# Parts of a head's sums loaded ahead of its attention and summed between projections; eight modulation tiles moved into the first layer's heads

## The chip, the cores and the metric

One core of a Trainium2 chip runs the whole program once per execution. The metric is the time of an execution on the device in microseconds. TensorE (PE) multiplies, VectorE (DVE) and ScalarE (ACT) do the elementwise work, GpSimd (POOL) helps, and SyncE (SP) issues all the DMAs of this kernel from one queue, in order. Every engine takes its instructions in one fixed order, which is set when the kernel is built: a scheduler simulates the program in time and lists, for each engine, what became ready first, by the order in which the program was written.

## The reference

Two layers over 1024 prompt tokens and 8 x 8 sample tokens, width 1024, 8 heads of 128. Each layer is a modulated RMS norm, a mixer with a gate path, an output projection and a gated residual. The modulation (shift, scale and gate, 3 x 1024 columns) is one product of the conditioning vectors with `ada_w`. Layer 0's mixer is a gated delta rule, layer 1's is attention in three dilated groups whose outputs are combined with weights from their log-sum-exponents:

```python
mod = einsum('bd,de->be', silu(c), ada_w) + ada_b
shift, scale, gate = split(mod, 3)
h = rms_norm(x, norm_g) * (1 + scale) + shift
x = x + gate * mixer(h)            # gated_delta_rule in layer 0, dilated attention in layer 1
...
for gi, (window, dil) in enumerate(((128, 1), (512, 4), (2048, 16))):
    o, lse = dilated_attn(q[gi], k[gi], v[gi], window, dil)
wts = softmax(stack(lses))         # over the three groups
o = sum(wts * stack(outs))         # the "sum" of a head
y = (o * silu(z)) @ w_out
```

## The kernel before, in words

A projection (`project`) is one tile of 128 output columns over all 1088 tokens: three chunks of 384, 384 and 320 tokens, each 24 products (8 blocks of the depth, times three products of the split operands: high by high, high by low, low by high). The weights come in by `wraw` (512 KB, two buffers in turn), ACT rounds them to `whi` and DVE or POOL subtracts to get `wlo` (two buffers each). A chunk's result stands in one of two PSUM banks `pp` until it is copied out.

A modulation tile (`ada_tile`) is 128 columns of `ada_w`: eight products written as 16 PE instructions with the conditioning vectors (L153), a copy by ACT (L155), a folding product (L160) and a bias by DVE (L166 to L170). Its 512 KB of weights come through `wraw` too. 24 such tiles stand in a list, and each convolution projection of layer 0's heads (24 of them, `conv_tile`, all but one) calls `ada.pump(1)`, which runs one tile. The last eight tiles, the gates of layer 1, were loaded through a pool of their own, `ap` (L142), and run at the end of layer 0, one behind each of eight blocks of the last modulation (`modulate`, L1086).

In layer 0 the scheduler gives PSUM banks named `ps` (two) in the order of the program. The program's order at the start is: the key projection of head 0 with its system (`stage_k`), its query and value projections (`stage_qv`), the key projection of head 1, and then the scans.

Layer 1 runs four pairs of heads; in each pair the groups g = 2, 1, 0, and in each group the two heads (a = 0, 1): three projections (v, k, q), then `attention`, which yields block by block. PE fills the waits of one head's attention with the next head's projections. After each projection come `qk.pump`, `pv.pump` (the sample tokens' work) and `cmb.pump(2)`. The outputs of groups 2 and 1 go to DRAM (`gscr`). When a head's group 0 is done, `combine` is put into `cmb`: for each half of the tokens it loads the two parts into two buffers `stgc` (L1254), does the sum on DVE and ACT (L1257 to L1275), transposes it on PE (L1279), copies it back into a `stgc` buffer (L1281) and stores it to `oscr` (L1282). The transposes are ordered behind the newest product of a projection (`newest[0]`). The gate path (`z_head`) reads `oscr` at the end of the layer.

Of the kernel before, what the change touches and what calls it, by code (L numbers as in the profile page):

```python
# [8 lines left out]
F32 = mybir.dt.float32  # L9
# [5 lines left out]
P = 128  # L15
# [27 lines left out]
def kernel(ctx, tc, I, O):  # L43
# [58 lines left out]
    def wraw(src, n=P):  # L102
        t = wp.tile([P, KD, P], F32, name="wraw", bufs=2)
        SY.dma_start(out=t[:, :, :n], in_=src.rearrange("(k p) n -> p k n", p=P))
        return t
# [30 lines left out]
                        next(woven[0], None)  # L136
            cb(ci, acc)

    def ada_load(layer, ct, pool, ahead):
        src = I["ada_w"][layer, :, ct * P:(ct + 1) * P]  # L140
        t = pool.tile([P, KD, P], F32, name="aw", bufs=ahead)
        SY.dma_start(out=t, in_=src.rearrange("(k p) n -> p k n", p=P))  # L142
        return t

    def ada_tile(layer, ct, w):
        ada_fold(layer, ct, ada_rows(w))

# [92 lines left out]
            if not self.todo:  # L240
                self.credit = 0.0

    def ada_tiles(pool, todo):
        def load(i):
            layer, ct = todo[i]
            return ada_load(layer, ct, pool, 2) if pool else wraw(I["ada_w"][layer, :, ct * P:(ct + 1) * P])
        w = load(0) if pool else None
        for n, (layer, ct) in enumerate(todo):
            nxt = load(n + 1) if pool and n + 1 < len(todo) else None
            ada_tile(layer, ct, w if pool else load(n))  # L250
            w = nxt
            yield

    ada = Units()
    ada.todo.append(ada_tiles(None, [(0, c) for c in range(16, 24)] + [(1, i + o) for i in range(8) for o in (8, 0)]))


    W0 = I["a_w_in"][0]
# [290 lines left out]
    def conv_tile(t, dst):  # L549
        w = wsplit(wraw(W0[:, t * P:(t + 1) * P]), G if 8 <= t < 16 else V)  # L550
        prev = [None]

        def cb(ci, acc):
            cn = CHUNKS[ci][1]
            xin = sb.tile([P, 387], F32, name="xin", bufs=2)
            if ci == 0:
                G.memset(xin[:, 0:3], 0.0)
            else:
                G.tensor_copy(out=xin[:, 0:3], in_=prev[0][:, 384:387])
            prev[0] = xin  # L560
            if ci < 2:
                A.copy(out=xin[:, 3:3 + cn], in_=acc[:, :cn])
                W = cn
            else:
                A.copy(out=xin[:, 3:259], in_=acc[:, :256])
                xs = xin[:, 259:347].rearrange("p (b x) -> p b x", x=11)
                G.tensor_copy(out=xs[:, :, 0:3], in_=scT[:, t, :].rearrange("p (b i) -> p b i", i=3))
                A.copy(out=xs[:, :, 3:11], in_=sview(acc[:, 256:320]))
                W = 344
                cst = sb.tile([P, 27], F32, name="cst", bufs=2)  # L570
                G.tensor_copy(out=cst[:, 0:3], in_=xin[:, 256:259])
                G.tensor_copy(out=cst[:, 3:27].rearrange("p (b i) -> p b i", i=3), in_=xs[:, :, 8:11])
                ct = acc[:27, 320:320 + P]
                PE.transpose(ct, cst, ident)
                cso = sb.tile([27, P], F32, name="cso", bufs=2)
                V.tensor_copy(out=cso, in_=ct)
                SY.dma_start(out=conv_p[:, t * P:(t + 1) * P], in_=cso[0:3, :])
                SY.dma_start(out=conv_s[:, t * P:(t + 1) * P], in_=cso[3:27, :])
            ca = sb.tile([P, 387], F32, name="ca", bufs=2)
            A.activation(out=ca[:, :W], in_=xin[:, 0:W], func=AF.Copy, scale=cwT[:, 0, t:t + 1])  # L580
            for i in range(1, 4):
                stt(ca[:, :W], xin[:, i:i + W], cwT[:, i, t:t + 1], ca[:, :W], ALU.mult, ALU.add)
            th = xin
            A.activation(out=th[:, :W], in_=ca[:, :W], func=AF.Tanh)
            c0 = CHUNKS[ci][0]
            if ci < 2:
                stt(dst[:, c0:c0 + cn], th[:, :cn], 1.0, ca[:, :cn], ALU.add, ALU.mult)
            else:
                stt(dst[:, c0:NP], th[:, :256], 1.0, ca[:, :256], ALU.add, ALU.mult)
                v1 = th[:, 259:347].rearrange("p (b x) -> p b x", x=11)[:, :, 0:8]  # L590
                v2 = ca[:, 259:347].rearrange("p (b x) -> p b x", x=11)[:, :, 0:8]
                stt(sview(dst[:, NP:]), v1, 1.0, v2, ALU.add, ALU.mult)
        project(w, hh, hl, cb)
        if t != 8:
            ada.pump(1)

    def banks_natural(src):
        out = []
# [409 lines left out]
    first.close()  # L1008
    set_banks(ctx, ps=3, lv=2, sc=1)

    aps = ExitStack()
    ap = aps.enter_context(tc.tile_pool(name="ap", bufs=1, reuse_waits="tile"))
    zp = ExitStack()
    zpool = zp.enter_context(tc.tile_pool(name="zp", bufs=1, reuse_waits="tile"))
    oh[7], ol[7] = (zpool.tile([P, T], F32R, name=n) for n in ("oh7", "ol7"))
# [47 lines left out]
    x1scr = [dr.tile([P, T], F32, name=f"x1scr{j}") for j in range(KD)]  # L1063
    x1 = [Columns("hh", F32) for _ in range(KD)]
    hh, hl = new_h()
    ada.todo.append(ada_tiles(ap, [(1, c) for c in range(16, 24)]))
    with tc.tile_pool(name="mid", bufs=1, reuse_waits="tile") as mp:
        def norm(qs, b0, b1):
            rn = col_stats(qs, b0, b1)
            rB = mp.tile([P, WIDE], F32, name="rB")  # L1070
            row_bcast(rB, rn, b0, b1)
            return rB

        def post(j):
            SY.dma_start(out=x1scr[j][:, :WIDE], in_=x1[j][:, :WIDE])

        def post2(j):
            SY.dma_start(out=x1scr[j][:, WIDE:], in_=x1[j][:, WIDE:])
            modulate(1, j, x1[j], rB, mp, hh, hl, 0, WIDE, True)
        qs = out_project(mp, 0, I["a_w_out"][0], xscr, x1, oh, ol, post, PASSES[0])  # L1080
        rB = norm(qs, 0, WIDE // P)
        qs = out_project(mp, 0, I["a_w_out"][0], xscr, x1, oh, ol, post2, PASSES[1])
        rB = norm(qs, WIDE // P, NC + 1)
        for j in range(KD):
            modulate(1, j, x1[j], rB, mp, hh, hl, WIDE, T, j % 2 and j < KD - 1)
            ada.pump(1)  # L1086
    zp.close()
    aps.close()
    l0.close()


# [45 lines left out]
    Z = [sd.tile([P, ZW * n], F32, name=f"Z{g}").rearrange("p (b x) -> p b x", b=2 * NB)  # L1137
         for g, n in enumerate((1, 4, 8))]
    for t in Z:
        V.memset(t, 0.0)  # L1140
    odS = sd.tile([P, 512], F32, name="odS")
    G.memset(odS, 0.0)
    comb = sd.tile([P, 4, NL], F32, name="comb")
# [18 lines left out]
    def proj_tile(g, part, h, dst, dsts):  # L1162
        col = ((part * NG + g) * NH + h) * P
        w = wsplit(wraw(W1_[:, col:col + P]))

        def cb(ci, acc):
            c0, cn = CHUNKS[ci]
            n = cn if ci < 2 else cn - NS
            todo = [(perm(dst, g, c0, n), pin(acc, g, n))]
            if ci == 2:  # L1170
                todo.append((dsts[:, h % 2, :], acc[:, n:cn]))
            for o, i in todo:
                if part == 0:
                    A.activation(out=o, in_=i, func=AF.Copy, scale=-SCALE)
                elif part == 1:
                    A.copy(out=o, in_=i)
                else:
                    V.tensor_copy(out=o, in_=i)  # L1178
        project(w, hh, hl, cb)

    def to_natural(src, nat, blocks, eng):
# [59 lines left out]
                A.copy(out=stg[:, b - 3:b + 1, 0:P], in_=v3(ob))  # L1241
            yield

    def combine(h, X0):

        for half in range(2):
            yield from combine_half(h, X0, half * 4)

    def combine_half(h, X0, n0):

        X = [X0[:, n0:n0 + 4, :]]
        for g in (1, 2):
            t = sb.tile([P, 4, 130], F32, name="stgc", bufs=2)
            SY.dma_start(out=t, in_=gscr[g - 1][h].rearrange("(n p) e -> p n e", p=P)[:, n0:n0 + 4, :])  # L1254
            X.append(t)
        yield
        d = sb.tile([P, NG, 4], F32, name="cd", bufs=1)  # L1257
        mm = sb.tile([P, 4], F32, name="cm", bufs=1)
        t = sb.tile([P, NG, 4], F32, name="ct", bufs=1)
# [11 lines left out]
        for n in range(4):  # L1271
            o = X[0][:, n, 0:P]
            A.activation(out=o, in_=o, func=AF.Copy, scale=d[:, 0, n:n + 1])
            for g in (1, 2):
                stt(o, X[g][:, n, 0:P], d[:, g, n:n + 1], o, ALU.mult, ALU.add)  # L1275
        yield
        tb = bank()
        for n in range(4):
            t = PE.transpose(tb[:, n * P:(n + 1) * P], X[0][:, n, 0:P], ident)  # L1279
            order_after(t, newest[0], "the sum is ready behind the products before")  # L1280
        A.copy(out=X[1][:, :, 0:P], in_=v3(tb))  # L1281
        SY.dma_start(out=oscr[h][:, n0 * P:(n0 + 4) * P].rearrange("p (n q) -> p n q", q=P), in_=X[1][:, :, 0:P])  # L1282

    def wide(tag, bufs, name=None, dtype=F32):

# [204 lines left out]
    for hp in range(4):  # L1490
        smd, vnew = [None] * NG, [None] * NG
        nmd = sd.tile([P, 4], F32, name="nmd", bufs=2)
        for g in (2, 1, 0):
            qTs, kTs, vTs = (sb.tile([P, 2, NS], F32, name=n, bufs=3) for n in ("qTs", "kTs", "vTs"))
            for a in range(2):
                h = 2 * hp + a
                vT = wide("vT", 1)
                kT = wide("kT", 2)
                qT = wide("qT", 2)
# [20 lines left out]
                if g == 1:  # L1520
                    SY.dma_start(out=scr.rearrange("(j p r) e -> p r j e", j=2, p=P),
                                 in_=stg.rearrange("p (r j) e -> p r j e", j=2))
                elif g == 2:
                    dv = scr.rearrange("(m rp r2) e -> r2 m rp e", rp=8, r2=2)
                    for r2 in range(2):
                        SY.dma_start(out=dv[r2], in_=stg[64 * r2:64 * r2 + 64])
                else:
                    cmb.todo.append(combine(h, stg))
                    cmb.pump(1)
        if hp < 3:  # L1530
            qk.todo.append(after(hp, smd, nmd, vnew))
# [70 lines left out]
```

## Time and profile before

| what | us |
|---|---|
| three runs, median (lowest to highest) | 2420.28 (2412.72 to 2430.17) |
| the profiled execution | 2412.29 |
| its span | 2410.6 |
| PE busy | 2250.9 (93%) |
| weight loads into PE busy | 2116.5 (88%) |
| DVE, ACT, POOL busy | 1375.5, 937.6, 257.6 |
| mean granted clock of PE | 0.962 |

By the order of time: to about 60 us the norm and modulation of layer 0; to about 835 its heads and gates; to about 970 its output projection and the norm and modulation of layer 1; to about 2235 the heads of layer 1; then gates and output. A matmul's end in the profile is modelled and overlaps the next one's start, so a busy PE is not PE at its peak. "[idle before <-releaser]" is how long the engine stood still just before the instruction, and what it had waited for.

### The profile page before, as it was taken

To read this page: it belongs to the slowest core of one execution; us is meant where nothing else is said; L and a number is where in the kernel's file an instruction comes from. 1 tells how busy PE (TensorE), PEld (TensorE's weight loads), DVE (VectorE), ACT (ScalarE), POOL (GpSimd) and SP (SyncE) were. 2 spreads that over 40 slices of the span, in tenths; PEclk is the share of its full clock that TensorE was granted. 3 is DMA by queue.
4 is the path that set the end of the run, shared out by engine and by line. 5 is a ranking of instruction groups with operands and counts; after the bars stand their busy time and mean duration, and the time that the engine had idled before them with its cause. 6 is when DMAs were issued, how large, how long until landed. Compare 5 with 4: busy or idle time off the path is not lost.

```text
span 2410.6 us, 43253 instructions
## 1 busy us (share of the span) xinstructions
PE 2250.9 (93%) x16647; PEld 2116.5 (88%) x16647; DVE 1375.5 (57%) x3414; ACT 937.6 (39%) x2477; POOL 257.6 (11%) x418
## 2 busy tenths in 40 slices
PE   7899889999999998999998999899998999999998
PEld 5788778788888997999898999899998999989897
DVE  6678767867784437336733555434655336375334
ACT  5445445455443325233233332333323333234234
POOL 2213322333221103100000000000000000000000
PEclk9889989899999999999999999999999999999998
DMA  9223222223333445448822697535966349786634
GB/s 314 69 74 86 76 68 76 79 69 91 79 87 89 120 149 162 131 146 265 272 66 71 218 301 246 167 100 183 332 222 211 98 143 337 198 267 180 203 101 149
DMA packets 482255, 379.42 MB, mean 157 GB/s; under 512 B 46206, under 2 KB 457071, under 8 KB 482048
## 3 DMA queue, kind: packets, MB, share of 16 engines
q1 hardware_dynamic: 482048, 376.65, 51.6%
q8 instruction: 131, 2.15, 0.4%
q14 instruction: 76, 0.62, 0.1%
HBM read 322.31 MB, written 54.27 MB: 156 GB/s over the span
## 4 chain that ended last, share of the span: by engine, by line
PE 65%; DMA 11%; DVE 11%; issue 7%; ACT 3%; POOL 1%; SPq 1%; POOLq 0%; ACTq 0%; DVEq 0%
PE pp L129 47%; PE ps L1238 2%; PE ps L1220 2%; DMA DT<-gcscr 2%; PE sc L1438 2%; DMA wraw<-in_a_w_in_dram 2%; DVE vtmp L713 2%; DMA qb<-qscr 1%; PE ps L1184 1%; DVE pr L1389 1%; PE ps L1229 1%; DVE ca L72 1%; DMA oscr<-stgc 1%; PE ps L153 1%; DMA out_y_p_dram<-yn 1%
## 5 line engine op out<-in xcount | busy, mean ns | idle before, releaser
L129 PE MATMUL pp<-hh,whi 128*128 128x384 f32 (+1 forms) x2688 | 914.3, 341 | 14.5 <-DVE vT L1178 5.8
L129 PE MATMUL pp<-hl,whi 128*128 128x384 f32 (+1 forms) x2688 | 904.0, 336 | 1.3 <-POOL hl L214 1.3
L129 PE MATMUL pp<-hh,wlo 128*128 128x384 f32 (+1 forms) x2688 | 900.8, 335 | 2.0 <-DVE wlo L111 2.0
L129 PEld LDWEIGHTS pp<-hh,whi 128*128 128x128 f32 x2688 | 512.5, 191 | 29.8 <-DVE vT L1178 8.5
L129 PEld LDWEIGHTS pp<-hl,whi 128*128 128x128 f32 x2688 | 512.8, 191 | 6.6 <-issue 1.9
L129 PEld LDWEIGHTS pp<-hh,wlo 128*128 128x128 f32 x2688 | 511.3, 190 | 7.7 <-issue 2.9
L111 DVE TENSOR_TENSOR wlo<-wraw,whi 128x1024 fp32r<-128x1024 f32 x136 | 171.2, 1259 | 131.3 <-ACT whi L110 130.5
L110 ACT CAST whi<-wraw 128x1024 fp32r<-128x1024 f32 x144 | 150.7, 1046 | 230.0 <-PE pp L129 148.2
L1225 ACT ACTIVATE sm<-sm,stg 128x128 f32<-128x128 f32 (+1 forms) x192 | 86.6, 451 | 340.4 <-DVE stg L1223 299.8
L1389 DVE TENSOR_TENSOR pr<-kc,qb 128x1024 f32<-128x1024 f32 x128 | 154.9, 1218 | 85.2 <-DMA qb<-qscr 55.7
L1379 DVE TENSOR_REDUCE ST<-pr 128x8 f32<-128x1024 f32 x128 | 153.7, 1213 | 1.1
L438 POOL TENSOR_TENSOR ol<-zo,oh 128x384 fp32r<-128x384 f32 x9 | 9.1, 1013 | 1311.4 <-ACT oh L437 1291.2
L72 DVE SCALAR_TENSOR_TENSOR ca<-xin,cwT,ca 128x384 f32<-128x384 f32 (+1 forms) x216 | 129.0, 601 | 7.1 <-ACT ca L580 5.9
L1223 DVE CUSTOM_DVE_ANT_0 sm<-ps,mA 128x256 f32<-128x256 f32 (+1 forms) x128 | 48.3, 377 | 139.4 <-PE ps L1220 138.2
L1238 PE MATMUL ps<-vnat,pT 128*128 128x128 f32 x560 | 97.1, 281 | 8.1 <-DVE pT L1234 6.4
L713 DVE TENSOR_TENSOR vtmp<-Vi,Mi 128x2 f32<-128x2 f32 (+30 forms) x248 | 99.0, 399 | 4.2 <-POOL so L88 0.7
L1238 PEld LDWEIGHTS ps<-vnat,pT 128*128 128x128 f32 x560 | 86.1, 190 | 14.3 <-issue 4.8
L1220 PE MATMUL ps<-kT,qT 128*128 128x128 f32 (+1 forms) x384 | 93.5, 325 | 1.2 <-DVE stg L1223 1.2
L1232 ACT COPY pT<-ps 128x256 f32<-128x256 f32 (+1 forms) x96 | 32.4, 337 | 119.3 <-PE ps L1229 118.4
L72 DVE SCALAR_TENSOR_TENSOR hh<-pp,GT,xr 128x384 f32<-128x384 f32 (+1 forms) x48 | 27.4, 571 | 82.4 <-PE pp L129 78.7
L129 PE MATMUL pp<-oh,whi 128*128 128x384 f32 (+1 forms) x216 | 71.7, 333 | 2.7 <-DVE zt L72 2.7
L129 PE MATMUL pp<-oh,wlo 128*128 128x384 f32 (+1 forms) x216 | 71.9, 334 | 1.5 <-DVE wlo L111 1.5
(449 smaller groups left out, 3556.1 us busy)
## 6 DMA issues: line engine op xcount, KB each, us to landing
qb<-qscr SPq DMA_DIRECT2D x128, 512.0 KB
kc<-in_cache_kv_w_dram SPq DMA_DIRECT2D x104, 512.0 KB
vc<-in_cache_kv_w_dram SPq DMA_DIRECT2D x104, 512.0 KB
wraw<-in_b_w_in_dram SPq DMA_DIRECT2D x80, 512.0 KB
wraw<-in_a_w_in_dram SPq DMA_DIRECT2D x32, 512.0 KB
wraw<-in_ada_w_dram SPq DMA_DIRECT2D x24, 512.0 KB
stgc<-gscr SPq DMA_DIRECT2D x32, 260.0 KB
aw<-in_ada_w_dram SPq DMA_DIRECT2D x8, 1024.0 KB
```

The lines of the kernel that those rows point to most:

```text
L72: return (eng or V).scalar_tensor_tensor(out=out, in0=in0, scalar=scalar, in1=in1, op0=op0, op1=op1)
L110: A.copy(out=hi, in_=raw)
L111: (eng or V).tensor_tensor(out=lo, in0=raw, in1=hi.bitcast(F32), op=ALU.subtract)
L129: mm = PE.matmul(acc[:, :cn], lhsT=a[:, k, :], rhs=b[k][:, c0:c0 + cn], start=(n == 0), stop=(n == 3 * KD - 1))
L713: V.tensor_tensor(out=tv, in0=Vi[:, :na, :w], in1=Mi[:, :w, c].unsqueeze(1).broadcast_to([P, na, w]), op=ALU.mult)
L1220: PE.matmul(sv, lhsT=qT[:, b * P:(b + 1) * P], rhs=kT[:, k0:k0 + w], start=True, stop=True)
L1223: V.tensor_tensor_reduce(out=sm[:, :w], in0=sv, in1=mk, scale=1.0, scalar=3e38, op0=ALU.add, op1=ALU.min, accum_out=stg[:, b, 128:129])
L1225: A.activation(out=sm[:, :w], in_=sm[:, :w], func=AF.Exp, scale=-1.0, bias=stg[:, b, 128:129], accum_out=stg[:, b, 129:130])
L1238: PE.matmul(ob[:, (b % 4) * P:(b % 4 + 1) * P], lhsT=pT[:, i * P:(i + 1) * P], rhs=vnat[:, k0 // P + i, :], start=(i == 0), stop=(i == w / ...
L1379: V.tensor_reduce(out=sv[:, n:n + 4, :], in_=pr.rearrange("p (n a e) -> p n a e", a=2, e=P), op=ALU.add, axis=AX.X)
L1389: V.tensor_tensor(out=out, in0=k, in1=q, op=ALU.mult)
L1438: mm = PE.matmul(od[32 * j:32 * j + 8, f * P:(f + 1) * P], lhsT=Z[g][:, a * NB + 2 * j + c, 8 * k:8 * k + 8], rhs=vc[:, j, a * P:(a + 1) * P],
```

## The change

- `combine` is put into `cmb` before the head's group 0 is projected, with an empty box. Its first step (after the projections of the head, or after the first one) loads the parts of the first half; it then yields until the head's own output is in the box. The sum of the first half follows directly behind the attention in the program, its transposes behind the next projection; the loads of the second half follow these, two more yields stand between, so its sum comes behind the second projection and its transposes behind the third.
- The eight gate tiles of layer 1 join the list of the 24; the calls behind three projections at the start (t = 0 and 16, query and value of head 0, and t = 9, key of head 1) run three tiles instead of one, 29 calls in all, and the last three tiles run where all that is left is run (`ada.pump(100)`, where one was left before). The pool `ap` goes.
- The tiles `Z` are cleared by POOL instead of DVE, and the value copies of the first projected head of layer 1 (group 2, head 0) are done by ACT instead of DVE.

```diff
-    def ada_load(layer, ct, pool, ahead):
...
-    ada.todo.append(ada_tiles(None, [(0, c) for c in range(16, 24)] + [(1, i + o) for i in range(8) for o in (8, 0)]))
+    ada.todo.append(ada_tiles([(0, c) for c in range(16, 24)] + [(1, i + o) for i in range(8) for o in (8, 0)]
+                              + [(1, c) for c in range(16, 24)]))
...
         if t != 8:
-            ada.pump(1)
+            ada.pump(3 if t in (0, 16, 9) else 1)
...
-    ada.todo.append(ada_tiles(ap, [(1, c) for c in range(16, 24)]))
...
             modulate(1, j, x1[j], rB, mp, hh, hl, WIDE, T, j % 2 and j < KD - 1)
-            ada.pump(1)
...
     for t in Z:
-        V.memset(t, 0.0)
+        G.memset(t, 0.0)
...
-                    V.tensor_copy(out=o, in_=i)
+                    (A.copy if (g, h) == (2, 0) else V.tensor_copy)(out=o, in_=i)
...
-    def combine(h, X0):
-        for half in range(2):
-            yield from combine_half(h, X0, half * 4)
...
+    def combine(h, box):
+        def load(n0):
+            parts = []
+            for g in (1, 2):
+                t = sb.tile([P, 4, 130], F32, name="stgc", bufs=2)
+                SY.dma_start(out=t, in_=gscr[g - 1][h].rearrange("(n p) e -> p n e", p=P)[:, n0:n0 + 4, :])
+                parts.append(t)
+            return parts
+        parts = load(0)
         yield
+        while not box:
+            yield
+        for n0 in (0, 4):
+            X = [box[0][:, n0:n0 + 4, :]] + parts
+            add_up(X)
+            yield
+            tb = bank()
+            for n in range(4):
+                t = PE.transpose(tb[:, n * P:(n + 1) * P], X[0][:, n, 0:P], ident)
+                order_after(t, newest[0], "the sum is ready behind the products before")
+            A.copy(out=X[1][:, :, 0:P], in_=v3(tb))
+            SY.dma_start(out=oscr[h][:, n0 * P:(n0 + 4) * P].rearrange("p (n q) -> p n q", q=P), in_=X[1][:, :, 0:P])
+            if n0 == 0:
+                parts = load(4)
+                yield
+                yield
+            yield
...
                 h = 2 * hp + a
+                if g == 0:
+                    box = []
+                    cmb.todo.append(combine(h, box))
...
                 else:
-                    cmb.todo.append(combine(h, stg))
+                    box.append(stg)
                     cmb.pump(1)
```

`add_up` is the body of the sum as it was (L1257 to L1275).

## Rows read from the trace of the kernel before

**Rows 1.** Page, part 1: busy us, share of span, instructions.
```profile
PE 2250.9 (93%) x16647; PEld 2116.5 (88%) x16647; DVE 1375.5 (57%) x3414; ACT 937.6 (39%) x2477; POOL 257.6 (11%) x418
```
**Rows 2.** PE's waits, 985 to 2235: us in total, times, longest.
```profile
PE ps L1279 <- DVE stg L72: 31.8, 5, 8.5
...
PE ps L1279 <- ACT knew L1326: 2.4, 1, 2.4
```
**Rows 3.** Order of time, PE: start us, us, instruction.
```profile
1291.43 0.45 PE L1279 MATMUL ps<-ident,stg 128*128 128x128 f32 x1 [6.04 <-DVE stg L72]
...
1544.71 0.44 PE L1279 MATMUL ps<-ident,stg 128*128 128x128 f32 x1 [8.33 <-DVE stg L72]
1544.95 1.91 PE L1184 MATMUL ps<-ident,vT 128*128 128x128 f32 x8
...
1908.56 0.45 PE L1279 MATMUL ps<-ident,stg 128*128 128x128 f32 x1 [4.62 <-DVE stg L72]
```
**Rows 4.** Order of time, SP, ACT and DVE beside these stalls.
```profile
1535.86 0.37 SPq L1282 DMA_DIRECT2D oscr<-stgc  x1
1538.38 0.36 SPq L1254 DMA_DIRECT2D stgc<-gscr  x1
...
1536.42 0.59 ACT L1241 COPY stg<-ps 128x512 f32<-128x512 f32 x1
1543.23 1.28 ACT L1273 ACTIVATE stg<-stg,cd 128x128 f32<-128x128 f32 x4 [1.18 <-DVE cd L1270]
...
1541.29 0.17 DVE L1261 TENSOR_TENSOR cm<-cm,stgc 128x4 f32<-128x4 f32 x1 [5.10 <-DMA stgc<-gscr]
...
1899.50 0.59 ACT L1241 COPY stg<-ps 128x512 f32<-128x512 f32 x1 [2.89 <-PE ps L1238]
```
**Rows 5.** Stage table, all work: window, us, busy by engine, granted clock, DMA.
```profile
1544.00:1546.00 2.00, 1.29 (x6) 1.32 (x7) 1.88 (x8) 0.50 (x2) 0.00 (x0) 0.50 0.00 0
...
1548.00:1550.00 2.00, 2.00 (x14) 2.00 (x15) 0.79 (x4) 0.57 (x3) 0.00 (x0) 0.94 0.61 182
```
**Rows 6.** Stage table of the seam: PE, PEld, DVE, ACT, POOL; then L129 alone.
```profile
951.90:971.60 19.70, 11.50 (x140) 8.17 (x129) 13.70 (x51) 7.67 (x25) 4.73 (x12) 0.65 0.72 212
...
951.90:971.60 19.70, 0.95 (x4) 0.69 (x5) 0.65 0.72 212
```
**Rows 7.** Order of time in the seam, PE, DVE and SP.
```profile
956.26 0.64 PE L153 MATMUL ps<-aw,cT 128*32 128x128 f32 x16 [2.51 <-DMA aw<-in_ada_w_dram]
...
951.97 0.49 DVE L72 SCALAR_TENSOR_TENSOR tmp<-hh,SC,rB 128x256 f32<-128x256 f32 x1 [0.28 <-ACT rB L226]
...
969.41 1.48 DVE L1178 COPY vT<-pp 128x384 f32<-128x384 f32 x2
...
952.11 13.93 SPq L142 DMA_DIRECT2D aw<-in_ada_w_dram  x6
```
**Rows 8.** Stage table, projections (L129) alone: window, us, PE, PEld, clock, DMA.
```profile
89.00:101.70 12.70, 11.41 (x65) 10.24 (x63) 1.00 0.32 61
...
101.70:123.00 21.30, 0.00 (x0) 0.00 (x0) 0.56 0.41 97
244.00:265.00 21.00, 0.00 (x0) 0.04 (x1) 0.83 0.23 64
```
**Rows 9.** Order of time in the seam, POOL clearing and DVE beside it.
```profile
966.21 0.32 POOL L1103 MEMSET mA<- 128x256 f32 x1
...
966.62 0.47 DVE L72 SCALAR_TENSOR_TENSOR tmp<-hh,SC,rB 128x256 f32<-128x256 f32 x1
```
**Rows 10.** Chain that ended last, 116 to 124: start us, us, what.
```profile
117.02 1.01 PE ps L153 x16
...
118.09 4.05 DMA wraw<-in_a_w_in_dram
...
122.16 1.04 ACT whi L110
```
**Rows 11.** Order of time, SP's queue at the start.
```profile
32.60 2.87 SPq L104 DMA_DIRECT2D wraw<-in_a_w_in_dram  x1
```

More of the change, by code (lines that the diff above doesn't have):

```diff
@@ L137, in project @@
             cb(ci, acc)
-    def ada_load(layer, ct, pool, ahead):
[L140 to L143, printed above, removed]
     def ada_tile(layer, ct, w):
@@ L241, in pump, with ada_tiles @@
                 self.credit = 0.0
[L243 to L251, printed above, removed]
+    def ada_tiles(todo):
+        for layer, ct in todo:
+            ada_tile(layer, ct, wraw(I["ada_w"][layer, :, ct * P:(ct + 1) * P]))
             yield
     ada = Units()
-    ada.todo.append(ada_tiles(None, [(0, c) for c in range(16, 24)] + [(1, i + o) for i in range(8) for o in (8, 0)]))
+    ada.todo.append(ada_tiles([(0, c) for c in range(16, 24)] + [(1, i + o) for i in range(8) for o in (8, 0)]
+                              + [(1, c) for c in range(16, 24)]))
     W0 = I["a_w_in"][0]
@@ L1009 @@
     set_banks(ctx, ps=3, lv=2, sc=1)
-    aps = ExitStack()
-    ap = aps.enter_context(tc.tile_pool(name="ap", bufs=1, reuse_waits="tile"))
     zp = ExitStack()
@@ L1085 @@
             modulate(1, j, x1[j], rB, mp, hh, hl, WIDE, T, j % 2 and j < KD - 1)
-            ada.pump(1)
     zp.close()
-    aps.close()
     l0.close()
@@ L1242, in attention, with add_up @@
             yield
-    def combine(h, X0):
-        for half in range(2):
-            yield from combine_half(h, X0, half * 4)
[L1249 to L1255, printed above, removed]
-        yield
+    def combine(h, box):
[7 more added lines that the diff above has]
+        parts = load(0)
+        yield
+        while not box:
[15 more added lines that the diff above has]
+            yield
+    def add_up(X):
         d = sb.tile([P, NG, 4], F32, name="cd", bufs=1)
@@ L1275, in combine_half @@
                 stt(o, X[g][:, n, 0:P], d[:, g, n:n + 1], o, ALU.mult, ALU.add)
[L1276 to L1282, printed above, removed]
     def wide(tag, bufs, name=None, dtype=F32):
```

## Prediction

> **What bounds the kernel now.** I read the page first: TensorE (PE) is busy 93% of the span, VectorE (DVE) 57%, and the weights' loads into the array 88% [rows 1]. So what counts is where PE stands still, and how long it runs at 1.2 GHz after it. The idle-time view of PE over the second layer's heads (985 to 2235 us) then names one line: the transposes of the head sums, L1279, wait 31.8 us on DVE's sum in five places and 2.4 us on ScalarE (ACT) in one [rows 2]. These 34.2 us are six stalls, one at the second half of each of the first six heads' sums (near 1238, 1291, 1544, 1601, 1851 and 1908 us). The order-of-time views of PE and of the other engines around one stall show the chain [rows 3, 4]. PE runs out of other work at 1536.4 and stands until 1544.71; right behind in its queue lie the eight transposes of the next head's values (L1184), which need no sum. What it waits for: the first half's result leaves by DMA at 1535.86, the second half's part can only be loaded into that buffer at 1538.38, DVE's sum starts at 1541.29 when it has landed, and the first transpose follows 3.42 us later. In the stage table the clock is at 0.50, the 1.2 GHz level, behind the stall, and back at 0.94 only from 1548 [rows 5]. So 1544.7 to about 1548.3 runs at half speed and costs another 1.8 us.
>
> The second place is the seam between the layers. In 951.9 to 971.6, of 19.7 us only 0.95 us of PE is projection [rows 6]: it does eight gate tiles of the modulation (and waits for their loads, 2.51 us in the row shown) while DVE modulates the last columns, and DVE then copies the first two chunks of the new projection, at 969.41, behind all that [rows 7].
>
> The third place is where the gate tiles go. Between 101.7 and 123 us PE has no projection at all, and 89 to 101.7 holds most of one [rows 8].
>
> **The change, part by part.**
> *Sums.* The number of instructions is the same: per head four loads of parts, two sums, eight transposes, two stores. Moved are the loads of the first half (ahead of the head's attention) and each sum (to one projection ahead of its transposes). A store-and-load cycle took 1535.86 to 1541.29, 5.4 us [rows 4]; a projection is 72 matmuls, and 65 of them took 12.7 us [rows 8]. The DMA leg is then covered in both halves. Left is that the second sum needs the last blocks of the attention, whose copy (L1241) ends at 1537.0 [rows 4], 0.6 us after the stall begins. If PE's order stays as it is, the transposes could come 1.5 to 3.5 us behind that copy: 1.5 when only the scaling and adding are left (ACT's first scaling at 1543.23 to the transpose at 1544.71), 3.5 when the whole sum is. That leaves 2 to 4 us of the stalls of this kind (those at 1291, 1544 and 1851). For the other three (1238, 1601, 1908) the copy came long before, as at 1899.50 against a stall from 1903.9 to 1908.56 [rows 3, 4], and nothing or 0.6 us is left. So at least 34.2 - 13 = 21 us go, and all 34.2 if the next head's transposes are ordered ahead. On the clock: the five stalls of 4.3 us and over are each followed by a slow stretch like that of rows 5, some 2 us apiece, 10 in all; two of them go for certain (4 us). Together 25 to 44; I take 36, nearer the upper end, because the sum's numbers no longer wait for a DMA and only the adding is left when the copy lands.
> What could come in its place: SP's queue now waits once more per pair of heads, when the next head's first parts want the buffer that the store of the head before still reads (1535.86 to 1538.38, 2.5 us [rows 4]). Behind that load in the queue stand the weights of the next projection, issued a projection ahead, so 2.5 us of 12.7 are covered. Nothing is charged; if the cover fails it is 4 times 2.5 = 10 us, and DVE's splits would be late next.
>
> *Seam.* Eight tiles go from here: eight loads of 512 KB, 128 matmuls, eight ACT copies, 16 folding matmuls and eight DVE additions. The two first value chunks are copied by ACT rather than behind DVE's modulation. What still has to run is DVE's modulation: its 13.70 us of work in the window less the 1.48 us of value copies is 12.2 us, with the tiles' additions still in it, so from 951.97 to 964.2 at the latest if DVE doesn't wait [rows 6, 7]. The third chunk, which started at 971.6, then starts at least 7.4 us sooner; as its products follow the modulation block by block, and the next projection's first chunk can run meanwhile, the end may move by up to 18.75 us (all of the window that was no projection). I take 12: 971.6 to 964.2, and the chunk's own time mostly run under the modulation. The cache loads, which stood behind the six gate loads in SP's queue (from 952.11 on for 13.9 us), come earlier; PE does not wait for them here, so that is worth nothing.
>
> The Z tiles are cleared by GpSimd (POOL) rather than DVE, which had no wait from it: nothing either way. The nearest row: while POOL cleared masks from 966.21 on, a two-input operation of DVE took 0.47 us at 966.62, and one of the same shape with POOL idle 0.49 at 951.97 [rows 7, 9]. The Trainium skill, GPSIMD Engine Reference, section Specifications, says that POOL shares its way into SBUF with VectorE and contends with DVE instructions that have two SBUF inputs, with no exception for a clear. By that rule the clearing would be taken from the 12: some 2 us (an estimate, 1664 columns at the row's 0.32 us for 256), which makes the sum 2378. By the row it takes nothing, and the row decides.
>
> *Gate tiles in the first layer's heads.* 32 tiles instead of 24 share two weight buffers with the projections. Three calls take three tiles each, six more, and two more are flushed at the end. A tile costs PE 1.0 us here and there [rows 10], 8 us, mostly beside other engines' waits. The buffers cost more. Before, the third projection's weights were loaded at 32.60 [rows 11], since only one tile stood ahead of it, and it ran 89 to 101.7. That one tile's products ran only at 117.02, when the first head's system had left it a PSUM bank; the buffer came free at 118.09, and the next weights took 4.05 us and a cast of 1.04 [rows 10]. With three tiles ahead, the third projection's weights wait for the second tile, after 118.1. So a projection of 12.5 us moves from a time when PE was free to one behind 123 us, and the next two triples each add about one more tile-and-load wait, some 4 us: about 20 us of backlog at 160 us. It can be worked off where PE has no projection to do, as in 244 to 265 (x0 [rows 8]). Bounds: 0 (all absorbed by the scan chain that paces the heads) and 24; I take 12, half the backlog and 2 for the flushed tiles.
>
> Sum: -36 - 12 + 12 = -36 us against the profiled execution's 2412.3: 2376. That execution lies 8 us under the median of the three runs (2420.28, from 2412.72 to 2430.17), so the same share off the median would be 2384; I say 2380.
>
> **Rivals.**
> 1. The sum is still late, because the attention ends as PE runs dry. For it: the copy at 1536.42 against 1536.4. Against it: three of six stalls had the copy early. Price: 25 instead of 36 goes: 2387 (2395 beside the median).
> 2. The early backlog isn't worked off. For it: the first heads' PE rows are dense after 125. Against: the holes of rows 8. Price 24 instead of 12: 2388 (2396).
> 3. Slower than before: the first layer's weight buffers. If each of the six extra tiles puts a whole matmul, load, cast and split in series (1.0 + 4.05 + 1.04 + 1.2 or more, about 7.5) on the path, that is 45, with the displaced projection 58; gains are 48, so it ends at 2422 (2430). It decides from 48 us of early cost on.
> 4. It doesn't do what it says: PE's order puts the transposes behind another late wait and the stalls only change their cause; then only the seam and the tiles count, 2412.
>
> **How the numbers follow.** Forecast 0.60, rival 1 0.15, rival 2 0.12, rival 3 0.07, rival 4 0.06. About 1% (24 us, below 2396 or above 2444) is what a measurement of this kernel can tell from no change. Faster: nearly all of the forecast and half of rivals 1 and 2, 0.70. Same: 0.25. Slower: the far part of rival 3, 0.05. Range: low is all stalls, the better seam and no early cost but the flush, 2412 - 44 - 18 + 2 = 2352; high is 2412 - 25 - 7 + 24 = 2404, and 8 for the median: 2412. The likeliest case alone lies between 2360 and 2394.
>
> **What would show it.** Sums right: L1279 waits under 13 us in all, and the clock stays at 1.00 behind the heads' ends. Seam right: no gate tile after 835, the first value copy on ACT, the third chunk done by 966 on before's scale. Tiles: the third projection starts after 118 instead of 89, and the stage from 60 to 836 us is longer by about 12. The forecast is wrong if L1279 is still the first of PE's waits, or if the first layer's heads grow by over 24 us.

## The result: 0.9% slower

| | before | after |
|---|---|---|
| median, same chip | 2417.72 us (12 runs) | 2437.76 us (12 runs) |
| ratio | | 1.0092 (95%: 1.0070 to 1.0113) |
| profiled execution | 2412.29 us | 2435.22 us |
| its span | 2410.6 us | 2433.5 us |
| column scales of the norm ahead of layer 1: last copy of `rB` starts | 951.5 us | 982.3 us |
| third chunk of layer 1's first projection starts | 971.6 us | 995.9 us |

2380 was predicted, with a range of 2352 to 2412; it came out outside it and on the other side. The column scales (`rB`, the norm's factor of each token) end the first layer here, and the start of the third chunk ends the seam. These two landmarks split the 22.9 us between the spans into the three places of the prediction. The first layer loses 30.8. The seam, from the column scales to the third chunk, shrinks from 20.1 to 13.6 and gives back 6.5. The 1439.0 us behind it become 1437.7, where the sums should have given 36.

(In after, lines below the modulation code have moved: the sums' transposes are L1248, their copy L1250, their store L1251, the loads of parts L1235, the values' transposes L1168, the gate tile's products L147, the seam's value copies L1162.)

**The sums.** PE's waits after, 985 to 2260 us (total, times, longest), answer to [rows 2]:

```profile
PE ps L1248 <- DVE stg L72: 34.4, 6, 8.5
```

The same six stalls with the same sum. One of them, in order of time on SP, PE, ACT and DVE, beside [rows 3, 4]:

```profile
1552.34 0.37 SPq L1235 DMA_DIRECT2D stgc<-gscr  x1
1560.97 0.37 SPq L1251 DMA_DIRECT2D oscr<-stgc  x1
1563.38 0.48 SPq L1235 DMA_DIRECT2D stgc<-gscr  x1
...
1559.72 0.60 PE L1248 MATMUL ps<-ident,stg 128*128 128x128 f32 x4
...
1569.96 0.45 PE L1248 MATMUL ps<-ident,stg 128*128 128x128 f32 x1 [8.46 <-DVE stg L72]
1570.20 1.06 PE L1168 MATMUL ps<-ident,vT 128*128 128x128 f32 x4
...
1560.36 0.59 ACT L1250 COPY stgc<-ps 128x512 f32<-128x512 f32 x1
...
1550.92 1.39 DVE L72 SCALAR_TENSOR_TENSOR stg<-stgc,cd,stg 128x128 f32<-128x128 f32 x5
1566.54 0.17 DVE L1263 TENSOR_TENSOR cm<-cm,stgc 128x4 f32<-128x4 f32 x1 [5.24 <-DMA stgc<-gscr]
```

The first half's sum is ready at 1552.3. Its transposes stand in PE's queue behind the projections that the scheduler put ahead, and run at 1559.72. ACT copies their result into the buffer of one *part* (1560.36), and the store out of it starts at 1560.97. Of the second half's two parts one is loaded at 1552.34, as soon as its buffer is read; the other wants the buffer being stored from, and is issued at 1563.38. DVE has it at 1566.54, PE goes on at 1569.96. Nothing of this is a wait for the *first* half's parts, which is the load that the change moved.

**The first layer.** SP's queue, loads of weights, beside [rows 11] and the load at 118.09 in [rows 10]:

```profile
28.69 6.98 SPq L104 DMA_DIRECT2D wraw<-in_ada_w_dram  x2
112.80 0.39 SPq L104 DMA_DIRECT2D wraw<-in_ada_w_dram  x1
115.19 0.39 SPq L104 DMA_DIRECT2D wraw<-in_a_w_in_dram  x1
117.68 19.34 SPq L104 DMA_DIRECT2D wraw<-in_ada_w_dram  x3
137.13 0.52 SPq L104 DMA_DIRECT2D wraw<-in_a_w_in_dram  x1
```

Two gate tiles take both weight buffers at 28.69; the third projection's weights follow at 115.19 instead of 32.60, the fourth's at 137.13 instead of 118.09, and the next two at 163.93 and 171.37 instead of 135.60 and 147.19. Projections (L129) in the windows of [rows 8]:

```profile
89.00:101.70 12.70, 0.00 (x0) 0.00 (x0) 0.75 0.62 90
101.70:123.00 21.30, 2.41 (x8) 2.08 (x9) 0.51 0.50 129
244.00:265.00 21.00, 13.14 (x69) 10.99 (x69) 0.94 0.20 47
```

The hole at 244 is filled, as the prediction had it: the ninth projection ends only 6 us later than before (282.0 against 275.7). But the fourth, fifth and sixth, the key projection of the second head and its query and value, end 17, 35 and 35 us later. The first head's last state leaves 5 us later and the second's 26 us later (346.2 to 372.5), and from the third head to the eighth the states stay 27 to 30 us late.

### The profile page after: what moved, and what is told of

It reads as the page before. It is cut to its first block, busy times and chain, and to the rows that moved or that the text cites. A ratio compares the mean times of both kernels' runs of the same rounds, so it can differ in the third digit from the quotient of the medians.

```text
span 2433.5 us, 43226 instructions
## 1 busy us (share of the span) xinstructions
PE 2273.0 (93%) x16647; PEld 2137.1 (88%) x16647; DVE 1374.0 (56%) x3407; ACT 944.3 (39%) x2481; POOL 253.1 (10%) x421
## 4 chain that ended last, share of the span: by engine, by line
PE 65%; DVE 12%; DMA 11%; issue 6%; ACT 4%; POOL 1%; SPq 1%; POOLq 0%; ACTq 0%; DVEq 0%
PE pp L129 45%; PE ps L1222 2%; PE ps L1204 2%; DVE pr L1384 2%; PE sc L1433 2%; DMA qb<-qscr 2%; DMA DT<-gcscr 1%; DMA wraw<-in_a_w_in_dram 1%; PE ps L1168 1%; DVE vtmp L702 1%; PE ps L1213 1%; DMA kc<-in_cache_kv_w_dram 1%; DVE ca L72 1%; PE ps L147 1%; DMA out_kv_s_dram<-knew 1%
## 5 line engine op out<-in xcount | busy, mean ns | idle before, releaser
L129 PE MATMUL pp<-hh,whi 128*128 128x384 f32 (+1 forms) x2688 | 919.9, 343 | 25.7 <-ACT vT L1162 12.5
L129 PE MATMUL pp<-hl,whi 128*128 128x384 f32 (+1 forms) x2688 | 907.7, 338 | 0.3 <-POOL hl L208 0.3
L129 PE MATMUL pp<-hh,wlo 128*128 128x384 f32 (+1 forms) x2688 | 904.2, 337 | 0.7 <-DVE wlo L111 0.7
L129 PEld LDWEIGHTS pp<-hh,whi 128*128 128x128 f32 x2688 | 516.4, 192 | 40.7 <-ACT vT L1162 12.8
L129 PEld LDWEIGHTS pp<-hl,whi 128*128 128x128 f32 x2688 | 516.0, 192 | 5.4 <-POOL hl L208 0.8
L129 PEld LDWEIGHTS pp<-hh,wlo 128*128 128x128 f32 x2688 | 515.1, 192 | 4.4 <-issue 1.4
L129 PE MATMUL pp<-oh,whi 128*128 128x384 f32 (+1 forms) x216 | 72.0, 333 | 2.7 <-DVE zt L72 2.7
L1207 DVE CUSTOM_DVE_ANT_0 sm<-ps,mG 128x128 f32<-128x128 f32 x64 | 18.4, 288 | 96.7 <-PE ps L1204 64.3
```

The lines of the kernel that those rows point to most:

```text
L129: mm = PE.matmul(acc[:, :cn], lhsT=a[:, k, :], rhs=b[k][:, c0:c0 + cn], start=(n == 0), stop=(n == 3 * KD - 1))
L1207: V.tensor_tensor_reduce(out=sm[:, :w], in0=sv, in1=mk, scale=1.0, scalar=3e38, op0=ALU.add, op1=ALU.min, accum_out=stg[:, b, 128:129])
```

## The experiments

Each ran beside the kernel before on the same chip; the ratios are to that. A single profile fixes the first layer's end only to some 8 us: e3_late, e6_late_back, e7_early_copy and e12_order have the same source there, and their column scales come at 956.9, 965.3, 960.4 and 959.9.

### Which part costs what

e1_sums is the kernel before with the head sums of the change alone (`combine` and its calls).

> The kernel before with only the new head sums (first half's parts loaded ahead of the attention, each sum a projection ahead of its transposes). Theory A (formed from the trace after): the program's order is a projection apart, but the queues are not; the second half's part still waits for the first half's store, the six stalls of PE stay at 34 us (30 to 38) and the time at 2418 (2410 to 2426). Prediction's theory: the DMA leg is covered, the stalls fall to under 13 us and the time to 2374 to 2393.

Measured: 2425.01 against 2421.19 us, ratio 1.0017 (0.9998 to 1.0036). PE's waits, 985 to 2235 us:

```profile
PE ps L1264 <- DVE stg L72: 32.8, 5, 8.5
...
PE ps L1264 <- ACT vnew L1338: 2.8, 1, 2.8
```

Before it was 31.8 and 2.4 [rows 2]. The new sums alone do nothing, neither good nor harm; the extra wait on SP's queue that the prediction looked for doesn't show.

e2_gates is the kernel before with the gate tiles moved alone:

```diff
-            ada.pump(1)
+            ada.pump(3 if t in (0, 16, 9) else 1)
...
-    ada.todo.append(ada_tiles(ap, [(1, c) for c in range(16, 24)]))
```

> The kernel before with only the gate tiles moved (32 tiles in the first layer's heads, three calls of three; none at the seam; sums, value copies and clears as before). Theory A: all that the change loses is here: the first layer's heads end 28 to 32 us later, the seam gives back 5 to 10, the time is 2436 to 2444. Rival B (the loss comes from the new sums or the other edits as well): 2405 to 2428.

Measured: 2447.58, ratio 1.0119 (1.0094 to 1.0144). So the loss is in the gate tiles, all of it, and somewhat more than theory A had: the median lies above its range, the first layer ends 40 us later (991.65) instead of 28 to 32, and the seam gives back less than its 5 to 10. In this profile the third chunk starts at 1007.61: a seam of 16.0 us without the tiles but with DVE's copies, against 20.1 before and 13.6 after. The tiles were worth 4.1 there, ACT's copies and the clears on POOL 2.4.

### Is it the place of the triples?

e3_late is the changed kernel with the triples in the fifth head.

```diff
-            ada.pump(3 if t in (0, 16, 9) else 1)
+            ada.pump(3 if t in (20, 4, 13) else 1)
```

> The changed kernel with the three triples of gate tiles issued in the fifth head (the values, queries and keys projections 20, 4, 13) rather than in the first (16, 0, 9). Theory A: what costs is that the triples stand ahead of the third projection while PE has nothing else to do, so the first head's end is back where it was before; the eight tiles then cost their own 8 to 15 us, and the time is 2412 to 2424. Rival C: a triple costs its weight buffers wherever it stands: 2432 to 2444.

Measured: 2421.14, ratio 0.9999 (0.9981 to 1.0018). The third projection's weights leave at 32.10 again. Stage table from 60 us to the column scales, all work: before, after, e3_late.

```profile
60.00:952.00 892.00, 823.32 (x6101) 741.38 (x6105) 626.22 (x1793) 410.12 (x1220) 218.97 (x350) 0.95 0.34 91
```

```profile
60.00:982.00 922.00, 854.05 (x6208) 766.93 (x6206) 627.22 (x1794) 414.34 (x1224) 212.54 (x349) 0.92 0.34 91
```

```profile
60.00:957.00 897.00, 830.74 (x6208) 746.92 (x6207) 628.85 (x1795) 411.69 (x1225) 215.78 (x349) 0.95 0.34 94
```

After and e3_late run the same 6208 matmuls there. After takes 25 us more, but PE stands idle hardly longer (68.0 us against 66.3, the window less the busy time): its *busy* time is 23.3 us longer, at a mean granted clock of 0.92 instead of 0.95. From 89 to 123 us the clock is 0.60 in after and 0.73 before. But that is bookkeeping, not yet a cause. All the loss is in place at the second head's last state (372.5 in after, 343.7 in e3_late); from there to the column scales after takes 609.8 us and e3_late 613.2, though its clock is 0.94 there against 0.96. And the next run has a longer busy time at a lower clock than e3_late, and loses nothing.

The late triples hold up the projections' loads as well. SP's loads of weights in e3_late, around the second of its triples:

```profile
420.27 0.38 SPq L104 DMA_DIRECT2D wraw<-in_a_w_in_dram  x1
420.77 0.52 SPq L104 DMA_DIRECT2D wraw<-in_ada_w_dram  x1
428.34 0.52 SPq L104 DMA_DIRECT2D wraw<-in_ada_w_dram  x1
452.03 0.38 SPq L104 DMA_DIRECT2D wraw<-in_ada_w_dram  x1
453.41 0.41 SPq L104 DMA_DIRECT2D wraw<-in_a_w_in_dram  x1
```

From one projection's load to the next, 33 us pass here, longer than behind a triple of after. Yet the last states of the third to the sixth head come up to 7 us earlier than before, and those of the last two only 6 and 4 us later. So a held load need not cost its time. That the projections of the fifth head run far enough ahead of the scans, and those of the second head do not, is inferred from this, not measured.

e8_noload keeps the triples in the first head and takes their loads away.

```diff
-            ada_tile(layer, ct, wraw(I["ada_w"][layer, :, ct * P:(ct + 1) * P]))
+            ada_tile(layer, ct, Resident() if n in (1, 2, 4, 5, 7, 8) else
+                     wraw(I["ada_w"][layer, :, ct * P:(ct + 1) * P]))
```

> The changed kernel, where the second and third gate tile of each of the three triples take a matrix that is already in SBUF in place of loaded weights: six loads of 512 KB less, the products, copies and folds of all tiles run as before (those six tiles' values are not the reference's). Theory A: the triples cost through the two weight buffers that they share with the projections, so the first layer's heads end within 8 us of the kernel before and the time is 2408 to 2420. Rival G: the tiles cost through their own work or their PSUM bank, wherever their weights lie: 2430 to 2442.

Measured: 2407.99 against 2415.38, ratio 0.9969 (0.9952 to 0.9986); the column scales come at 953.8. Its stage table, as above:

```profile
60.00:954.00 894.00, 842.78 (x6207) 758.96 (x6204) 616.87 (x1794) 412.50 (x1225) 215.34 (x349) 0.93 0.33 91
```

With all their products, copies, folds and PSUM banks, but without these loads, the triples in the first head cost nothing that shows, although PE is busy 12.0 us longer than in e3_late, at 0.93. So it is the loads and not the tiles' work. The run takes away the transfers together with their turns in the two buffers; that the turns are what counts is read from SP's rows of after, where each projection's load leaves only behind the last load of a triple.

e9_t0, e10_t16 and e11_t9 leave one triple in the first head, the other two late:

```diff
-            ada.pump(3 if t in (0, 16, 9) else 1)
+            ada.pump(3 if t in (0, 4, 13) else 1)
```

(16 or 9 in place of 0 in the other two.)

> The changed kernel with the triple behind the queries projection (0) left where it is and the other two in the fifth head (4 and 13). Theory A: the third projection's weights, which then wait for a tile that is only used near 118 us, are most of the loss: 2430 (2426 to 2440), the first head's third projection ends near 137 us and the layer's heads 18 to 30 us later than before. Rival H (each triple in the first head costs about a third of the loss): 2424 to 2430.

> As e9_t0, but it is the triple behind the values projection (16) that stays in the first head. Theory A: the third projection runs at 89 to 102 us again, the second head's keys projection (9) waits for one tile more: 2418 (2412 to 2426). Rival H: 2424 to 2430.

> As e9_t0, but it is the triple behind the second head's keys projection (9) that stays. Theory A: nothing waits for it that sets the end, 2418 (2410 to 2424). Rival H: 2424 to 2430.

Measured: 1.0028 (1.0009 to 1.0046), 1.0039 (1.0020 to 1.0059) and 1.0012 (0.9989 to 1.0034). Over e3_late that is some 7, 10 and 3 us, each to about 7 us either way by the two intervals; together 20, beside the 22 of the three at once (1.0092 against 0.9999), but too uncertain to show that they add up. All three medians lie in rival H's range (2424 to 2430). Theory A of e9_t0 did not come true: the triple that holds up the third projection is hardly most of the loss, and its column scales, at 960.0, are no later than those with all triples late. In e9_t0 that projection ends 33 us later than before and the next already only 5 us later: SP's rows show why.

```profile
113.39 0.39 SPq L104 DMA_DIRECT2D wraw<-in_a_w_in_dram  x1
115.84 0.37 SPq L104 DMA_DIRECT2D wraw<-in_ada_w_dram  x1
119.94 0.37 SPq L104 DMA_DIRECT2D wraw<-in_a_w_in_dram  x1
```

With no second triple behind it, the fourth projection's weights leave at 119.94, against 118.09 before. The reading that fits is that in after each triple keeps the *next* projection's load behind its own tiles, three times running, so that the second head's projections are never caught up. The shares of the single triples are open: the profile of e11_t9 shows layer 0 ending 19 us later than before, its median 3 us.

### What do the sums wait for?

e4_back is e1_sums with two edits:

```diff
             add_up(X)
+            if n0 == 0:
+                parts = load(4)
             yield
...
-            A.copy(out=X[1][:, :, 0:P], in_=v3(tb))
+            A.copy(out=X[0][:, :, 0:P], in_=v3(tb))
```

and the store reads X[0]: the transposed sum goes back into the head's own tile, so neither part's buffer is held by a store.

> The kernel before with the new head sums, and the transposed sum written back into the head's own tile rather than into the part's buffer, so that the second half's parts are loaded right behind the first sum (two buffers as before). Theory A: the store-and-load cycle between the halves is what PE waits for, so the stalls fall from 34 to 8 to 14 us (what is left waits for the last blocks of the attention) and the time to 2388 to 2402. Rival D: PE's order puts the transposes where the sum is late whatever the loads do: stalls 28 to 36 us, 2410 to 2426.

Measured: 2379.86, ratio 0.9826 (0.9800 to 0.9852), more than theory A had, with fewer stalls left. PE's waits, 985 to 2260 us, then one stall in order of time on SP, PE and ACT:

```profile
PE ps L1266 <- DVE stg L72: 6.4, 3, 2.1
...
1531.34 1.42 SPq L1251 DMA_DIRECT2D stgc<-gscr  x2
1541.02 0.36 SPq L1269 DMA_DIRECT2D oscr<-stg  x1
...
1543.69 0.30 PE L1266 MATMUL ps<-ident,stg 128*128 128x128 f32 x1 [2.15 <-DVE stg L72]
...
1541.58 0.59 ACT L1241 COPY stg<-ps 128x512 f32<-128x512 f32 x1
1542.20 1.28 ACT L1292 ACTIVATE stg<-stg,cd 128x128 f32<-128x128 f32 x4
```

Both parts of the second half are issued at 1531.34, ahead of the store. Three stalls are left, of 2.1 us each: the attention's last blocks are copied at 1541.58, scaled at 1542.20 and added. Stage table from the third chunk to the end, all work, before and e4_back:

```profile
971.60:2410.60 1439.00, 1370.06 (x9972) 1332.84 (x9972) 697.33 (x1480) 484.50 (x1159) 16.41 (x23) 0.97 0.62 192
```

```profile
975.80:2383.00 1407.20, 1363.45 (x9972) 1325.71 (x9972) 699.73 (x1480) 484.61 (x1159) 16.57 (x23) 0.99 0.63 196
```

The same 9972 matmuls take 31.8 us less: PE stands idle 25.2 us less (68.9 to 43.7, the window less the busy time) and is busy 6.6 us less, with the clock at 0.99 instead of 0.97. The sum's stalls alone are 27.8 us less (34.2 to 6.4); other waits grow a little. The medians differ by about 42. One profile of this stretch varies too: without the write-back (before, after, e1_sums, e3_late, e8_noload) it takes 1435.4 to 1451.4 us, with it (e4_back to e7_early_copy, e12_order) 1397.5 to 1407.2. The two edits were made together, so neither is priced by itself.

e5_after_back is the changed kernel with these two edits, e6_late_back has the late triples as well.

> The changed kernel, with only the transposed sum written back into the head's own tile and the second half's parts loaded right behind the first sum (as in e4_back). Theory A: the two places are independent, so it gains what e4_back gained (28 us by the stalls, 41 by the medians): 2396 (2388 to 2412), with stalls of 5 to 14 us. Rival D (the gain was tied to the order of the kernel before): 2425 to 2440.

> The changed kernel with both repairs: the triples of gate tiles in the fifth head (e3_late) and the sum written back (e4_back). Theory A: 2380 (2372 to 2392), no better than e4_back within what the runs can tell, since the seam gives about what the eight tiles cost in the heads. Rival E: the seam's 6.5 us shows once the sums no longer stall: 2366 to 2374.

Measured: 2396.11 against 2415.38, ratio 0.9917 (0.9888 to 0.9945), with L1250 at 6.4 us in three waits; and 2378.83, ratio 0.9848 (0.9824 to 0.9872). Each gains what theory A had, so sums and gate tiles are independent within what the runs can tell. The seam's gain doesn't show beside e4_back.

e12_order adds to e6_late_back that the second half's transposes are issued a projection later:

```diff
             if n0 == 0:
                 parts = load(4)
+            else:
+                yield
+                yield
             yield
```

> As e6_late_back, and the second half's transposes are issued one projection later, behind the next head's work. Theory A: the 6.4 us of stalls that are left in front of those transposes go to under 2, and with the clock behind them the time is 4 to 9 us under e6_late_back: 2368 to 2378. Rival D: PE stands still there for want of other work, so the stalls change their line and the time stays within 3 us of e6_late_back.

Measured: 2374.03 against 2421.82, ratio 0.9814 (0.9788 to 0.9840), the lowest of all, but its interval overlaps those of e4_back and e6_late_back. PE's waits, 930 to 2260 us, first two rows of e6_late_back, then one of e12_order:

```profile
PE ps L1250 <- DVE stg L72: 6.4, 3, 2.1
...
PE sc L1434 <- DMA vc<-in_cache_kv_w_dram: 1.9, 1, 1.9
```

```profile
PE sc L1437 <- DMA vc<-in_cache_kv_w_dram: 5.7, 3, 3.1
```

The transposes' wait on the sum is gone, but the wait for the cache loads grows by 3.8 us and that for the value copies by 1.9 (5.5 to 7.4). Its span is 5.0 us under that of e6_late_back, but the column scales come 5.4 us earlier (959.9 against 965.3), in a layer that the edit doesn't touch; from the third chunk to the end the two take 1398.8 and 1398.4 us. So the profiles speak for rival D: the stalls changed their line.

### What holds the seam?

PE's one long wait at the seam of after, and the copy that ends it:

```profile
994.84 0.24 ACT L203 CAST hh<-tmp 128x64 fp32r<-128x64 f32 x1
994.99 1.48 ACT L1162 COPY vT<-pp 128x384 f32<-128x384 f32 x2
...
995.85 0.64 PE L129 MATMUL pp<-hh,whi 128*128 128x320 f32 x1 [12.48 <-ACT vT L1162]
```

e7_early_copy gives that copy priority:

```diff
-                    (A.copy if (g, h) == (2, 0) else V.tensor_copy)(out=o, in_=i)
+                    if (g, h) == (2, 0):
+                        with tc.high_priority(offset=2000):
+                            A.copy(out=o, in_=i)
...
```

> As e6_late_back, and ScalarE's copies of the second layer's first value projection are given priority, so that they can stand ahead of its modulation work at the seam. Theory A: PE's 12 us wait for that copy at the seam shrinks to under 5, the third chunk of that projection ends with the modulation, and the time is 5 to 10 us under e6_late_back: 2362 to 2380. Rival F: the third chunk needs the modulation's last block anyway and the wait only changes its name: within 3 us of e6_late_back.

Measured: 2379.36, ratio 0.9849 (0.9819 to 0.9880), e6_late_back's. But the edit did not move the copy: it stands behind the last modulation cast in ACT's queue as in e6_late_back, and PE waits 12.2 us. So it tells nothing of an early copy; what keeps the scheduler from putting it ahead, and what that would bring, stays open.

## Why the prediction was wrong, step by step

Between the forecast of -36 us and the 22.9 us by which the profiled span grew lie 59: 34.7 are the sums, 18.8 the early gate tiles, 5.5 the seam.

- **The sums, -36: -1.3.** The reading of the stall was right down to the cycle (store, load, sum, transposes). The step that failed is "the DMA leg is then covered in both halves". It set a *program* distance, one projection between a load and its sum, against a *time* (12.7 us). But the queues are reordered: the first half's transposes run where the projections end, and the cycle starts there. And the leg belonged to a buffer, not to a load's place: the second half's part could not be loaded before the store had left, and the change still writes the transposed sum into that part's buffer. In the kernel before, the output operand of the copy in front of the store says so. The arithmetic itself held: with the buffer freed (e4_back) 28 of 34.2 us of stalls go, and what is left is 2.1 us behind the attention's last copy, as the prediction worked out (1.5 to 3.5). Stalls and clock, 25 to 44, hold both the 42 between the medians and the 31.8 between the profiles; the clock's part, put at 4 to 10, is 6.6.
- **The seam, -12: -6.5.** Below its bounds (7 to 18.75). DVE's modulation ends some 13 us after the column scales, as computed (12.2). The term took the third chunk to start with that end, at 964.2 on before's scale; that start came (13.6 us after the scales), but the chunk's own time did not run under the modulation, because the two copies that free its PSUM bank stand on ACT behind the modulation, where they had stood on DVE. What an earlier copy would give is open.
- **Early gate tiles, +12: +31.** The mechanism was right: the third projection starts after 118, its weights wait for the second tile. The step that failed is the size: "half the backlog". The backlog of 20 us at 160 us was about right (17 us for the fourth projection), then it grew to 35 for the fifth and sixth. The hole at 244 did take most of it up, 6 us being left at the ninth; but these three are the second head's own projections. Its last state came 26 us late, and no later head made that up. Filling a hole with projections did not bring the scans forward. The clock, which the term left out, was lower in that stretch (0.92 against 0.95 in e3_late), but how much of the 31 us it caused is not shown: e8_noload had 0.93 and lost nothing.
- **Flushed tiles, the clears on POOL:** no run separates them. The clears could not show a cost: most ran at 995.4, behind the modulation.
- **The rivals.** Rival 1 (the attention ends late) is what is left once the buffer is free: three stalls of 2.1 us. Rival 2 (the early backlog costs 24) came nearest to the measured 31, though not for its reason: the projections caught up, the scans did not. Rival 3 (the weight buffers) had the place and the mechanism, with a price of 45 to 58 against the 31 measured. It was to decide from 48 us on, but that threshold was the sum of two gains that didn't come. Rival 4 (sums do nothing) came true, with the old cause of the stalls rather than a new one. Rivals 3 and 4 were priced as alternatives; they came together.
- **What would show it:** the text named L1279 as PE's first wait and a first layer longer by over 24 us as signs of failure. Both are there.

## What to carry to other kernels

Before you move a load ahead, look at what frees its buffer: a buffer that is reused as the staging tile of a store is free only when the store is through (here the load left 2.4 us behind the store's start), however early the load stands in the program. An optional load that takes its turn in the buffers of the main stream holds up every main load behind it until a buffer is free again; put it where nothing waits for those loads. Here the same three triples cost 22 us more in the first head than in the fifth. And work off a backlog in your estimate only up to the chain that paces the stage: projections caught up here, the scan did not.

## What the runs showed of the hardware

While POOL subtracts two SBUF tiles, a DVE operation with two SBUF inputs that starts beside it ends 0.1 to 0.3 us after it, in three pairs out of three. At the seam of after, POOL and DVE in order of time:

```profile
985.44 1.01 POOL L208 TENSOR_TENSOR hl<-tmp,hh 128x320 fp32r<-128x320 f32 x1 [3.44 <-ACT hh L207]
...
985.65 0.88 DVE L195 TENSOR_TENSOR tmp<-hh,rB 128x64 f32<-128x64 f32 x1
987.24 0.22 DVE L195 TENSOR_TENSOR tmp<-hh,rB 128x64 f32<-128x64 f32 x1
```

The same operation takes 0.22 us 1.6 us later. Two more such pairs (0.77 for 0.22, 0.79 for 0.47) make it 1.5 us of the seam's modulation. The Trainium skill, SBUF — State Buffer, section "SBUF: two separate sides", says that the port pair shared by DVE and GpSimd is an exclusive lock for the whole instruction, and that a two-input DVE operation meets it only against a GpSimd operation that reads SBUF. The trace agrees on both: beside the subtraction 0.88 us for 0.22, and beside a clear, which reads nothing, the usual 0.47 for the longer form, in before at 966.62 [rows 9]. The clear shown there ends 0.1 us before that operation starts; the one that runs beside it is the third:

```profile
966.61 0.21 POOL L1111 MEMSET mdec<- 128x128 f32 x1
```
